# Modulation weights of a two-layer hybrid backbone: pages of four k tiles, selector matmuls for the block sums, other mixing rates

## The chip, the cores and the metric

The kernel runs on one core of one Trainium2 chip. The metric is the device time of one execution in microseconds. Lower is better. Before the change the median of three runs is 1393.65 us (1391.40 to 1397.22).

## What is computed

The reference is a backbone of two layers over 256 latent tokens and 256 context tokens of width 1024, in float32. Each layer has a mixing part (differential attention, a gated linear recurrence and a gated delta rule, four heads each, side by side) and a feed-forward part with a convolution over positions. Ahead of and behind each part the tokens are normalized and modulated. The modulation vectors are what the change is about:

```python
cond_lat = jax.nn.silu(c)[:, None, :]
cond_ctx = jax.nn.silu(c_ctx)
for layer in range(DEPTH):
    mod_l = jnp.split(cond_lat @ ada_w[layer] + ada_b[layer], 6, axis=-1)
    mod_c = jnp.split(cond_ctx @ ada_w[layer] + ada_b[layer], 6, axis=-1)
    p_l = split_cols(modulate(rms_norm(x, norm_g[layer, 0]), mod_l[0], mod_l[1]) @ w_in[layer])
    ...
    x = x + mod_l[2] * rms_norm(mix_l, norm_g[layer, 1])
    ff_l = conv_ffn(modulate(rms_norm(x, norm_g[layer, 2]), mod_l[3], mod_l[4]), ...)
    x = x + mod_l[5] * rms_norm(ff_l, norm_g[layer, 3])
```

So for each layer two vectors of 1024 numbers (one for the latent tokens, one for the context) are multiplied by a matrix of 1024 x 6144, some 25 MB, and a bias is added.

## The kernel before

Tokens lie along the free axis and channels along the 128 partitions. The large products are made of three matmuls each (lines 283 to 285 and 293 to 295), of a high and a low part of weights and activations: ScalarE makes the high part of a weight page (`whi`, line 269), VectorE or GpSimd the low part (`wlo`, line 273). A page is 128 x 1024 float32, 512 KB.

The modulation is computed in blocks of 512 output columns, twelve in a layer. What the first normalization of layer 0 needs (its blocks 0 to 3) is made at the start in eight units of 256 columns by `ada_unit` (line 330), in another form; the other twenty blocks are made by `ada` (line 307). A block reads four pages, each with two of the eight k tiles and 512 columns. The stationary operand is `cs`, the two condition vectors padded to 32 columns, so that a matmul fills only 32 of the 128 output rows. Its place among four column groups of the array is `g = k % 4` (line 316), so that one page fills groups 0 and 1 and the next one groups 2 and 3. When all eight k tiles are in, each group holds the sum over two of them. VectorE copies the bank to SBUF (line 320), four transposes turn it (line 323), a reduction over the four groups adds the partial sums (line 325), and a last instruction adds the bias and writes `mod` (line 326). `ada_unit` already works in the other way: pages of four k tiles and 256 columns (line 337), and a matmul with a selector (line 343), a constant of 128 x 2 that picks row 32 g + s of each group for stream s, so that the matmul adds the four groups itself.

The order of the work is set by generators that `weave` (line 1067) interleaves: each has a rate, and the one that has made the smallest share of its rate goes next. In the mixers of a layer (`mixers`, line 1089) these are the input projections, the delta rule (`gdn`), the recurrence (`hgrn`), attention (`da`) and the modulation blocks, with the rates `RATE[ly][0..4]`; `RATE[ly][5]` is the delta rule's in the stretch before. A scheduler then sets each engine's queue. Layer 0 makes its blocks 4 to 9 in the mixers and blocks 10, 11 and layer 1's blocks 0 to 3 as fill beside the out projection and the first up projections; layer 1 makes blocks 4 to 9 in its mixers and 10 and 11 as fill. The pages of the mixers' blocks use the four `raw` buffers, those of the fill the two `kq` buffers (line 1217).

The delta rule works on two halves of the tokens. For each, and for each of two head pairs, `gA` holds a decay matrix that GpSimd multiplies by beta (line 658), VectorE combines it with the keys' products `kk` (lines 668 to 671) and then solves a triangular system in six levels: matmuls `rt` and `dT` (line 602) with VectorE's updates of `gC` between them (lines 702 to 721). GpSimd also prepares `gF` (line 727) and `gB` (line 729), which are used behind the solve, and the recurrence's `K` (line 930). The level loop of the recurrence copies `K` on ScalarE (`kj`, line 911).

Of the kernel before, what the change touches and what calls it, by code (L numbers as in the profile page):

```python
# [17 lines left out]
AX = mybir.AxisListType  # L18
PSUM = bass.MemoryType.PSUM

P = 128
D = 1024
KT = 8
DEPTH = 2
# [17 lines left out]
    dict(mul=3, add=0, norm=3, lo=1, acc=0, dy=1, dx=8, wlo=2, nxt=2, fill=2, rate=5, hold=1),  # L42
    dict(mul=3, add=0, norm=3, lo=1, acc=0, dy=1, dx=0, wlo=2, nxt=0, fill=2, rate=5, hold=0),
)
RATE = ((121, 197, 32, 218, 37, 8), (53, 64, 15, 50, 5, 7))

GD_Q, GD_K, GD_V, GD_G = 0, 2, 4, 6
HG_Q, HG_G, HG_F, HG_I = 8, 10, 12, 16
# [4 lines left out]
def in_columns():  # L53
    base = np.cumsum([0, 512, 512, 512, 256, 256, 512, 256, 768, 8, 8, 256])
    daq, dak, dav, hgq, hgi, hgf, hgg, gdq, ga, gb, gdg = base[:11].tolist()
    starts = [gdq + 128 * i for i in range(6)] + [gdg, gdg + 128]
    starts += [hgq, hgq + 128, hgg, hgg + 128]
    starts += [hgf + 128 * i for i in range(4)] + [hgi, hgi + 128]
    starts += [dak + 128 * i for i in range(4)]
    starts += [dav + 128 * i for i in range(4)]  # L60
    starts += [daq + 128 * i for i in range(4)]
    ab = []
    for h2 in range(2):
        for kind in (ga, gb):
            for d in range(2):
                for hp in range(2):
                    ab.append(kind + d * 4 + hp * 2 + (h2 ^ hp))
    return starts, ab
# [21 lines left out]
def constants():  # L90
    c = np.zeros((P, C_N), np.float32)

    def put(name, a):
        o, w = C_OFF[name]
        c[:, o:o + w] = a

    i = np.arange(P)
    put("ident", np.eye(P))
    put("ones", 1.0)
    same = (i[:, None] // 64) == (i[None] // 64)  # L100
    put("bones", same)
    put("obones", ~same)
    pm = np.zeros((P, P))
    for m in range(2):
        for d in range(32):
            pm[m * 64 + d + 32, m * 64 + d] = -1.0
            pm[m * 64 + d, m * 64 + d + 32] = 1.0
    put("perm", pm)
    r, j = i[:, None] % 64, np.arange(64)[None]
    put("i64", r == j)  # L110
    big = np.float32(1e30)
    inc = np.concatenate([j >= r, j <= r], 1)
    strict = np.concatenate([j < r, j > r], 1)
    inc, strict = (np.concatenate([t[:, 64:], t[:, :64]], 1) for t in (inc, strict))
    put("inc2", inc)
    put("ninc2", -big * ~inc)
    put("pstr2", big * ~strict)
    hg = []
    for lev in range(LEVELS):
        b = 1 << lev  # L120
        sib = (r // (2 * b)) == (j // (2 * b))
        rl, jl = (r // b) % 2 == 0, (j // b) % 2 == 0
        hg.append(sib & (rl != jl))
    put("hgm", np.concatenate(hg, 1))
    n_freq = 16
    freq = np.float32(10000.0) ** (-np.arange(n_freq, dtype=np.float32) / np.float32(n_freq))
    tok = np.arange(256)
    ang = np.concatenate([(tok // 64).astype(np.float32)[:, None] * freq, (tok % 64).astype(np.float32)[:, None] * freq], -1)
    put("cos", np.cos(ang.T)[i % 32])
    put("sin", np.sin(ang.T)[i % 32])  # L130
    put("eps", EPS)
    put("one", 1.0)
    put("sel", i[:, None] % 32 == np.arange(2)[None])
    put("sel8", i[:, None] % 16 == np.arange(16)[None])
    return c
# [9 lines left out]
class Kernel:  # L145
# [161 lines left out]
    def ada(self, ly, blocks, tags=("raw",), bank="d"):  # L307
        nc = self.nc
        mod = self.mod[ly]
        for j in blocks:  # L310
            ps = self.bank(bank, "ada")
            for kc in range(4):
                w = self.load_raw(self.I["ada_w"][12 * ly + j - 4, kc], 1024, tags[kc % len(tags)]).rearrange("p (k n) -> p k n", k=2)
                for kk in range(2):
                    k = 2 * kc + kk
                    g = k % 4
                    nc.tensor.matmul(ps[32 * g:32 * g + 32, :], self.cs[:, k, :], w[:, kk, :], start=k < 4, stop=k >= 4,  # L317
                                     tile_position=(0, 32 * g))
            st = self.tmp("d2", "adas")
            nc.vector.tensor_copy(st, ps)  # L320
            ps2 = self.bank(bank, "ada2")
            for i in range(4):
                nc.tensor.transpose(ps2[:, 128 * i:128 * i + 128], st[:, i * 128:(i + 1) * 128], self.C("ident"))
            sm = self.small("adr", 8)
            nc.vector.reduce_sum(sm, ps2.rearrange("p (a g s) -> p a s g", a=4, g=4)[:, :, 0:2, :], axis=AX.X)
            nc.vector.tensor_tensor(
                mod[:, 4 * j:4 * j + 4, :], sm.rearrange("p (a s) -> p a s", s=2),
                self.V(ly, "adab", 4 * j, 4 * j + 4).unsqueeze(2).to_broadcast([P, 4, 2]), ALU.add)

    def ada_unit(self, u):  # L330
# [758 lines left out]
    def mixers(self, ly, hT, last, pending):  # L1089
        nc = self.nc  # L1090
        rate = RATE[ly]
        qlo = NCTX if last else 0
# [273 lines left out]
def pack(inp):  # L1366
    f = lambda a: np.ascontiguousarray(np.asarray(a, dtype=np.float32))
    A = {}
    x, ctx = f(inp["x"])[0], f(inp["ctx"])[0]
    tok = np.concatenate([ctx, x], 0)  # L1370
    A["xT"] = f(tok.reshape(NTOK, KT, P).transpose(2, 1, 0))
    cc = np.stack([f(inp["c_ctx"]), f(inp["c"])[0]], -1)
    A["cT"] = f(cc.reshape(KT, P, 2).transpose(1, 0, 2))
    A["consts"] = constants()
    starts, ab = in_columns()
    w = f(inp["w_in"]).reshape(DEPTH, KT, P, -1)
    A["w_in"] = f(np.stack([w[..., s:s + 128] for s in starts], 1).transpose(0, 1, 3, 2, 4)).reshape(DEPTH, N_IN, P, 1024)
    A["w_ab"] = f(w[..., ab].transpose(0, 2, 1, 3)).reshape(DEPTH, P, 128)
    w = f(inp["w_out"]).reshape(DEPTH, KT, P, KT, P)
    A["w_out"] = f(w.transpose(0, 3, 2, 1, 4)).reshape(DEPTH, KT, P, 1024)  # L1380
    w = f(inp["ffn_w_up"]).reshape(DEPTH, KT, P, 44, P)
    A["w_up"] = f(w.transpose(0, 3, 2, 1, 4)).reshape(DEPTH, 44, P, 1024)
    w = f(inp["ffn_w_down"]).reshape(DEPTH, 22, P, KT, P)
    for gi, (f0, fn) in enumerate(GROUPS):
        A[f"w_down{gi}"] = f(w[:, f0:f0 + fn].transpose(0, 3, 2, 1, 4)).reshape(DEPTH, KT, P, fn * P)
    w = f(inp["ada_w"]).reshape(DEPTH, 4, 2, P, 12, 512)
    A["ada_w"] = f(w.transpose(0, 4, 1, 3, 2, 5)).reshape(DEPTH * 12, 4, P, 1024)[4:]
    w = f(inp["ada_w"])[0].reshape(2, 4, P, 6, KT, P)[:, :, :, :2]
    A["ada_w0"] = f(w.transpose(4, 0, 2, 1, 3, 5)).reshape(KT, 2, P, 1024)
    v = np.zeros((DEPTH, P, V_N), np.float32)  # L1390

    def put(ly, name, a):
        o, wd = V_OFF[name]
        v[ly, :, o:o + wd] = a

    cols = lambda a: np.asarray(a).reshape(-1, P).T
    for ly in range(DEPTH):
        put(ly, "g", cols(inp["norm_g"][ly]))
        put(ly, "adab", cols(inp["ada_b"][ly]))
        put(ly, "subln", cols(inp["da_subln_g"][ly]))  # L1400
        put(ly, "lbl", cols(inp["hg_lb_logits"][ly]))
        put(ly, "hgn", np.tile(np.asarray(inp["hg_norm_g"][ly]), 2)[:, None])
        put(ly, "gdn", np.tile(np.asarray(inp["gd_norm_g"][ly]), 2)[:, None])
        put(ly, "cw", np.asarray(inp["gd_conv_w"][ly]).reshape(3, 6, P).transpose(2, 1, 0).reshape(P, 18))
        put(ly, "fw", np.asarray(inp["ffn_conv_w"][ly]).reshape(3, 44, P).transpose(2, 1, 0).reshape(P, 132))
        put(ly, "fb", cols(inp["ffn_conv_b"][ly]))
        for name, src in (("alog", "gd_a_log"), ("dt", "gd_dt_bias")):
            a = np.asarray(inp[src][ly]).reshape(2, 2, 2)
            a = np.stack([np.stack([a[:, hp, h2 ^ hp] for hp in range(2)], 1) for h2 in range(2)], 2)
            put(ly, name, np.concatenate([np.broadcast_to(a[:, :, h2].reshape(1, 4), (64, 4)) for h2 in range(2)], 0))  # L1410
    A["vec"] = v
    A["lam"] = f(np.broadcast_to(f(inp["da_lambda"]).reshape(DEPTH, 1, 256), (DEPTH, P, 256)))
    return A
# [17 lines left out]
```

## Time and profile before

| what | value |
|---|---|
| median of three runs | 1393.65 us (1391.40 to 1397.22) |
| the profiled execution's own time | 1397.04 us |
| span of that execution | 1395.3 us |
| mean granted TensorE clock | 0.974 |
| TensorE busy | 1298.6 us, 93% of the span |
| VectorE, ScalarE, GpSimd busy | 892.5, 658.9, 393.7 us |
| HBM read | 182.14 MB |

The profile is of one execution. The busy table tells which engine has least room. The windows give busy time, granted clock and DMA share of a stretch. The timeline lists instructions of an engine in order; neighbours of one line are put together as x4 or x16, with the time from the first start to the last end, so that the time to the next row's start is what they take of the engine. A float32 matmul shows as two records. The waits name who released an idle engine.

### The profile page before, as it was taken

The page shows a single profiled execution, that of the slowest core. Times are in us where ns is not written, and L with a number is a line of the kernel's source. Part 1 is how long each engine was busy: PE and PEld are TensorE (multiplying, and loading weights), DVE is VectorE, ACT ScalarE, POOL GpSimd, SP SyncE. Part 2 cuts the span into 40 slices and gives each one's busy share as a digit, 9 for nine tenths or more (in the row PEclk, how much of TensorE's full clock was granted, in tenths as well). Part 3 has the DMA queues.
Part 4 walks back from the last instruction along what each step waited for, and adds up shares of the span by engine and source line. Part 5 has one row for each costly group of instructions (what it writes and reads, how often), then busy time and mean ns, then how long its engine had stood idle before and what let it go on. Part 6 is the DMA issues. An engine that isn't in the chain of part 4 may idle for free.

```text
span 1395.3 us, 26653 instructions
## 1 busy us (share of the span) xinstructions
PE 1298.6 (93%) x10720; PEld 1048.0 (75%) x10720; DVE 892.5 (64%) x1722; ACT 658.9 (47%) x1189; POOL 393.7 (28%) x378
## 2 busy tenths in 40 slices
PE   5999997999989999999999997999989998999996
PEld 2768665666677678888888886997666765999995
DVE  3565657877647876434543559877697665776665
ACT  3364424444465544323432455675253354655553
POOL 1012014201046223201210266221241024655553
PEclk8999998999999999999999999999999999999998
DMA  8612443112335663323233234544221265455552
GB/s 300 211 46 91 167 165 139 32 47 76 107 121 189 207 217 115 104 92 105 91 101 96 82 122 135 173 145 155 95 103 34 106 243 181 139 183 185 189 167 76
DMA packets 56283, 185.96 MB, mean 133 GB/s; under 512 B 6368, under 2 KB 10464, under 8 KB 56160
## 3 DMA queue, kind: packets, MB, share of 16 engines
q1 hardware_dynamic: 56160, 184.27, 39.9%
q8 instruction: 84, 1.38, 0.4%
q14 instruction: 39, 0.32, 0.1%
HBM read 182.14 MB, written 2.10 MB: 132 GB/s over the span
## 4 chain that ended last, share of the span: by engine, by line
PE 74%; DVE 12%; ACT 5%; POOL 4%; issue 2%; DMA 2%; SPq 0%; DVEq 0%; POOLq 0%; ACTq 0%
PE up L284 8%; PE up L283 8%; PE up L285 8%; PE in L293 6%; PE in L294 5%; PE in L295 5%; PE dn L285 4%; PE dn L284 4%; PE dn L283 4%; PE ada L317 2%; DVE wlo L273 2%; PE sc L1035 2%; PE op L284 1%; PE op L283 1%; PE op L285 1%
## 5 line engine op out<-in xcount | busy, mean ns | idle before, releaser
L273 DVE TENSOR_TENSOR wlo<-raw,whi 128x1024 fp32r<-128x1024 f32 (+2 forms) x241 | 299.8, 1245 | 269.1 <-issue 90.4
L269 ACT CAST whi<-raw 128x1024 fp32r<-128x1024 f32 (+1 forms) x244 | 248.9, 1023 | 122.6 <-PE dn L285 99.0
L285 PE MATMUL up<-h,whi 128*128 128x256 f32 (+1 forms) x768 | 248.7, 324 | 1.3 <-DVE h L441 0.7
L283 PE MATMUL up<-h,whi 128*128 128x256 f32 (+1 forms) x768 | 248.3, 324 | 1.2 <-ACT h L438 1.1
L284 PE MATMUL up<-h,wlo 128*128 128x256 f32 (+1 forms) x768 | 248.0, 324 | 0.9 <-DVE wlo L273 0.9
L293 PE MATMUL in<-h,whi 128*128 128x512 f32 (+1 forms) x496 | 184.8, 373 | 2.2 <-DVE kq L481 2.2
L273 POOL TENSOR_TENSOR wlo<-raw,whi 128x256 fp32r<-128x256 f32 (+1 forms) x111 | 127.1, 1145 | 173.2 <-ACT whi L269 76.4
L294 PE MATMUL in<-h,wlo 128*128 128x512 f32 (+1 forms) x496 | 175.5, 354 | 0.0
L295 PE MATMUL in<-h,whi 128*128 128x512 f32 (+1 forms) x496 | 175.3, 354 | 0.0
L283 PEld LDWEIGHTS up<-h,whi 128*128 128x128 f32 x768 | 145.8, 190 | 19.6 <-issue 4.2
L285 PEld LDWEIGHTS up<-h,whi 128*128 128x128 f32 x768 | 145.9, 190 | 16.4 <-issue 1.7
L284 PEld LDWEIGHTS up<-h,wlo 128*128 128x128 f32 x768 | 145.9, 190 | 15.5 <-DVE wlo L273 1.9
L284 PE MATMUL dn<-gT,wlo 128*128 128x256 f32 (+1 forms) x400 | 127.6, 320 | 3.4 <-DVE wlo L273 3.4
L283 PE MATMUL dn<-gT,whi 128*128 128x256 f32 (+1 forms) x400 | 127.7, 320 | 2.7 <-ACT gT L300 2.7
L285 PE MATMUL dn<-gT,whi 128*128 128x256 f32 (+1 forms) x400 | 127.3, 320 | 0.5 <-POOL gT L302 0.5
L1262 POOL TENSOR_TENSOR u<-u 128x512 f32<-128x512 f32 (+1 forms) x44 | 44.4, 1010 | 278.3 <-DVE u L481 257.5
L293 PEld LDWEIGHTS in<-h,whi 128*128 128x128 f32 x496 | 96.2, 194 | 19.8 <-issue 5.4
L294 PEld LDWEIGHTS in<-h,wlo 128*128 128x128 f32 x496 | 96.2, 194 | 12.7 <-issue 3.5
L295 PEld LDWEIGHTS in<-h,whi 128*128 128x128 f32 x496 | 95.9, 193 | 12.3 <-issue 1.3
L477 ACT ACTIVATE u<-up,vec 128x256 f32<-128x256 f32 (+1 forms) x96 | 61.8, 644 | 75.2 <-PE up L285 75.2
L284 PEld LDWEIGHTS dn<-gT,wlo 128*128 128x128 f32 x400 | 76.7, 192 | 9.1 <-DVE wlo L273 4.0
L283 PEld LDWEIGHTS dn<-gT,whi 128*128 128x128 f32 x400 | 76.8, 192 | 8.2 <-ACT gT L300 3.1
(281 smaller groups left out, 2318.2 us busy)
## 6 DMA issues: line engine op xcount, KB each, us to landing
raw<-ada_w SPq DMA_DIRECT2D x96, 512.0 KB, 4.4
raw<-w_up SPq DMA_DIRECT2D x96, 512.0 KB, 3.5
raw<-w_in SPq DMA_DIRECT2D x68, 512.0 KB, 3.6
raw<-w_down SPq DMA_DIRECT2D x32, 512.0 KB, 3.5
raw<-w_out SPq DMA_DIRECT2D x24, 512.0 KB, 3.5
raw<-w_down SPq DMA_DIRECT2D x24, 384.0 KB, 3.1
x<-xT SPq DMA_DIRECT2D x16, 256.0 KB, 6.1
x_spill<-x SPq DMA_DIRECT2D x8, 128.0 KB, 2.0
```

Of the source, the lines that this page charges most:

```text
L269: nc.scalar.copy(hi[:, :cols], raw[:, :cols])
L273: e.tensor_sub(lo[:, a:b], raw[:, a:b], hi[:, a:b].bitcast(F32))
L283: nc.tensor.matmul(ps, wh[:, k, :], ah, start=first and k == ks[0], stop=False)
L284: nc.tensor.matmul(ps, wl[:, k, :], ah, start=False, stop=False)
L285: nc.tensor.matmul(ps, wh[:, k, :], al, start=False, stop=last and k == ks[-1])
L293: nc.tensor.matmul(ps, wh[:, k, :], ah, start=k == 0, stop=False)
L294: nc.tensor.matmul(ps, wl[:, k, :], ah, start=False, stop=False)
L295: nc.tensor.matmul(ps, wh[:, k, :], al, start=False, stop=k == n - 1)
L317: nc.tensor.matmul(ps[32 * g:32 * g + 32, :], self.cs[:, k, :], w[:, kk, :], start=k < 4, stop=k >= 4, tile_position=(0, 32 * g))
L477: nc.scalar.activation(dst, ps, AF.Identity, scale=w3[1], bias=bias)
L1035: nc.tensor.matmul(ps[:, :128 * nk], q[64 * m:64 * m + 64, a + 128 * qt:a + 128 * qt + 128], k[64 * m:64 * m + 64, :128 * nk], start=True, ...
L1262: self.nc.gpsimd.tensor_mul(us[0][:, lo:], us[0][:, lo:], us[1][:, lo:])
```

## The change

A page now holds four k tiles of 256 columns, one for each column group; four pages are two column halves by two sets of k tiles. The number and size of the pages stay. The matmuls of a block are chained by manual dependencies that set their order without a semaphore. The transposes and the reduction become four matmuls with the selector, and the bias is added straight from PSUM. Six of the twelve rates are set anew: layer 0's delta rule from 197 to 189, attention from 218 to 221, modulation from 37 to 19; layer 1's projections from 53 to 52, delta rule from 64 to 56, attention from 50 to 26.

```diff
-RATE = ((121, 197, 32, 218, 37, 8), (53, 64, 15, 50, 5, 7))
+RATE = ((121, 189, 32, 221, 19, 8), (52, 56, 15, 26, 5, 7))
...
             ps = self.bank(bank, "ada")
-            for kc in range(4):
-                w = self.load_raw(self.I["ada_w"][12 * ly + j - 4, kc], 1024, tags[kc % len(tags)]).rearrange("p (k n) -> p k n", k=2)
-                for kk in range(2):
-                    k = 2 * kc + kk
-                    g = k % 4
-                    nc.tensor.matmul(ps[32 * g:32 * g + 32, :], self.cs[:, k, :], w[:, kk, :], start=k < 4, stop=k >= 4,
-                                     tile_position=(0, 32 * g))
+            prev = []
+            for i in range(4):
+                half, kc = i // 2, i % 2
+                w = self.load_raw(self.I["ada_w"][12 * ly + j - 4, i], 1024, tags[i % len(tags)]).rearrange("p (k n) -> p k n", k=4)
+                for g in range(4):
+                    x = nc.tensor.matmul(ps[32 * g:32 * g + 32, 256 * half:256 * half + 256], self.cs[:, 4 * kc + g, :], w[:, g, :],
+                                         start=kc == 0, stop=kc == 1, tile_position=(0, 32 * g))
+                    prev = [self._dep(x, prev)]
             st = self.tmp("d2", "adas")
             nc.vector.tensor_copy(st, ps)
             ps2 = self.bank(bank, "ada2")
             for i in range(4):
-                nc.tensor.transpose(ps2[:, 128 * i:128 * i + 128], st[:, i * 128:(i + 1) * 128], self.C("ident"))
-            sm = self.small("adr", 8)
-            nc.vector.reduce_sum(sm, ps2.rearrange("p (a g s) -> p a s g", a=4, g=4)[:, :, 0:2, :], axis=AX.X)
+                nc.tensor.matmul(ps2[:, 2 * i:2 * i + 2], st[:, 128 * i:128 * i + 128], self.C("sel"), start=True, stop=True)
             nc.vector.tensor_tensor(
-                mod[:, 4 * j:4 * j + 4, :], sm.rearrange("p (a s) -> p a s", s=2),
+                mod[:, 4 * j:4 * j + 4, :], ps2[:, 0:8].rearrange("p (a s) -> p a s", s=2),
...
-    w = f(inp["ada_w"]).reshape(DEPTH, 4, 2, P, 12, 512)
-    A["ada_w"] = f(w.transpose(0, 4, 1, 3, 2, 5)).reshape(DEPTH * 12, 4, P, 1024)[4:]
+    w = f(inp["ada_w"]).reshape(DEPTH, 2, 4, P, 12, 2, 256)
+    A["ada_w"] = f(w.transpose(0, 4, 5, 1, 3, 2, 6)).reshape(DEPTH * 12, 4, P, 1024)[4:]
```

How the pages fall among other matmuls shows in TensorE's queue in the fill of layer 0. `up` is an up projection, `ada` a modulation block, the last names are the operands; x2 and x4 are neighbouring matmuls. Before, one of the blocks there:

```order
1875 L284 MATMUL up_4816<-h_4072,wlo_4813 128x256
1876 L317 MATMUL ada_4850<-raw_4851,cs 32x512
1877 L285 MATMUL up_4816<-h_4072,whi_4812 128x256
1878 L283 MATMUL up_4816<-h_4073,whi_4812 128x256
1879 L284 MATMUL up_4816<-h_4073,wlo_4813 128x256
1880 L285 MATMUL up_4816<-h_4073,whi_4812 128x256
1881 L317 MATMUL ada_4850<-raw_4851,cs 32x512
1882 L317 MATMUL ada_4850<-raw_4855,cs 32x512 x2
1883 L283 MATMUL up_4892<-h_4066,whi_4888 128x256
```

And a block at the same place with the change:

```order
1874 L317 MATMUL ada_4898<-raw_4899,cs 32x256 x4
1875 L317 MATMUL ada_4898<-raw_4905,cs 32x256 x4
1876 L283 MATMUL up_4946<-h_4102,whi_4942 128x256
...
1900 L283 MATMUL up_4989<-h_4102,whi_4985 128x256
1901 L317 MATMUL ada_4898<-raw_4911,cs 32x256 x4
1902 L284 MATMUL up_4989<-h_4102,wlo_4986 128x256
...
1910 L283 MATMUL up_4989<-h_4105,whi_4985 128x256
1911 L317 MATMUL ada_4898<-raw_4917,cs 32x256 x4
1912 L284 MATMUL up_4989<-h_4105,wlo_4986 128x256
```

The pages of a block stand apart in both orders. A page that stands alone was two matmuls of 512 columns and is now four of 256.

The second place is GpSimd's queue at the second half of layer 0's delta rule. Lines from 325 on are one lower in the changed file. The two numbers that `gA` and `gB` come with are the two head pairs. Before:

```order
26 L658 TENSOR_TENSOR gA_1983<-gA_1983,sbeta_640 128x512
27 L727 TENSOR_TENSOR gF_2725<-gB_1985,sbeta_640 128x512
28 L729 TENSOR_TENSOR gB_1985<-gB_1985,skd_676 128x256
29 L727 TENSOR_TENSOR gF_2725<-gB_1986,sbeta_640 128x512
30 L729 TENSOR_TENSOR gB_1985<-gB_1985,skd_676 128x256
31 L729 TENSOR_TENSOR gB_1986<-gB_1986,skd_676 128x256 x2
32 L658 TENSOR_TENSOR gA_1984<-gA_1984,sbeta_640 128x512
33 L930 TENSOR_TENSOR K_203_1175<-K_203_1175,F_202_1174 128x128x2x2 x2
```

With the change:

```order
26 L726 TENSOR_TENSOR gF_2702<-gB_1956,sbeta_640 128x512
27 L657 TENSOR_TENSOR gA_1954<-gA_1954,sbeta_640 128x512
28 L728 TENSOR_TENSOR gB_1956<-gB_1956,skd_676 128x256 x2
29 L657 TENSOR_TENSOR gA_1955<-gA_1955,sbeta_640 128x512
30 L929 TENSOR_TENSOR K_203_1175<-K_203_1175,F_202_1174 128x128x2x2 x2
31 L726 TENSOR_TENSOR gF_2702<-gB_1957,sbeta_640 128x512
32 L728 TENSOR_TENSOR gB_1957<-gB_1957,skd_676 128x256 x2
```

The second gA stood behind seven instructions of this half and now stands behind four; a gF, two gB and nothing else moved from ahead of it to behind it, a gF moved ahead of the first gA, and the pair of K now comes ahead of the second gF.

## Rows read from the trace of the kernel before

**Rows 1.** The page's first part: busy us, share of the span, instructions of each engine.
```profile
PE 1298.6 (93%) x10720; PEld 1048.0 (75%) x10720; DVE 892.5 (64%) x1722; ACT 658.9 (47%) x1189; POOL 393.7 (28%) x378
```

**Rows 2.** Busy us by stretch (from:to, length, engines, PEclk, DMA share, GB/s).
```profile
350.00:450.00 100.00, 89.97 (x826) 72.84 (x825) 59.01 (x132) 53.32 (x123) 38.02 (x36) 0.95 0.40 135
450.00:560.00 110.00, 105.13 (x644) 82.48 (x643) 78.84 (x123) 55.73 (x89) 29.71 (x27) 1.00 0.56 185
...
1000.00:1050.00 50.00, 44.90 (x459) 31.49 (x457) 45.20 (x108) 23.11 (x50) 21.09 (x18) 0.93 0.28 96
1050.00:1100.00 50.00, 46.47 (x610) 32.70 (x610) 38.56 (x109) 18.68 (x42) 3.99 (x4) 1.00 0.25 86
```

**Rows 3.** Timeline: an intact block and the next matmul (start us, us, engine, line).
```profile
147.11 1.92 PE L317 MATMUL ada<-raw,cs 128*32 128x512 f32 x16
...
148.97 0.68 PE L602 MATMUL rt<-gC,gA 64*64 64x64 f32 x16
```

**Rows 4.** TensorE's timeline: the first, one middle and the last separate page visit.
```profile
375.89 1.05 PE L317 MATMUL ada<-raw,cs 128*32 128x512 f32 x2
...
445.83 1.05 PE L317 MATMUL ada<-raw,cs 128*32 128x512 f32 x4
446.81 0.38 PE L284 MATMUL op<-mix,wlo 128*128 128x256 f32 x1
...
1181.92 3.16 PE L317 MATMUL ada<-raw,cs 128*32 128x512 f32 x8 [1.52 <-DMA raw<-ada_w]
```

**Rows 5.** TensorE's timeline at the start: one page of four groups, the next matmul.
```profile
37.77 0.64 PE L337 MATMUL ada<-raw,cs 128*32 128x256 f32 x8
38.34 0.50 PE L283 MATMUL in<-h,whi 128*128 128x512 f32 x1
```

**Rows 6.** TensorE's timeline: four transposes of a block, the next matmul.
```profile
176.21 0.60 PE L323 MATMUL ada<-consts,adas 128*128 128x128 f32 x4
176.57 0.47 PE L295 MATMUL in<-h,whi 128*128 128x512 f32 x1
```

**Rows 7.** TensorE's timeline: two selector matmuls; the same without the first record.
```profile
61.90 0.50 PE L343 MATMUL ada<-consts,adas 128*128 128x2 f32 x4
...
61.93 0.47 PE L343 MATMUL ada<-consts,adas 128*128 128x2 f32 x3
62.26 0.48 PE L283 MATMUL in<-h,whi 128*128 128x512 f32 x1
```

**Rows 8.** Instructions on the tile ada: VectorE's reduction (ns min/median/max).
```profile
L325 DVE TENSOR_REDUCE sadr<-ada x20: 142/191/193, 154.2 to 1186.6; 128x8 f32<-128x32 f32 x20
```

**Rows 9.** Waits of TensorE, 215 to 260 us: total us, times, longest.
```profile
PE rt L602 <- DVE gC L707: 8.3, 1, 8.3
PE wt L1052 <- ACT kj L911: 1.6, 1, 1.6
```

**Rows 10.** GpSimd's timeline, second half of layer 0's delta rule.
```profile
214.56 1.05 POOL L658 TENSOR_TENSOR gA<-gA,sbeta 128x512 f32<-128x512 f32 x1 [2.13 <-ACT gA L222]
215.56 3.70 POOL L727 TENSOR_TENSOR gF<-gB,sbeta 128x512 f32<-128x512 f32 x1
219.34 2.63 POOL L729 TENSOR_TENSOR gB<-gB,skd 128x256 f32<-128x256 f32 x1
221.93 2.02 POOL L727 TENSOR_TENSOR gF<-gB,sbeta 128x512 f32<-128x512 f32 x1
223.92 1.87 POOL L729 TENSOR_TENSOR gB<-gB,skd 128x256 f32<-128x256 f32 x3
225.75 1.04 POOL L658 TENSOR_TENSOR gA<-gA,sbeta 128x512 f32<-128x512 f32 x1
```

**Rows 11.** GpSimd's timeline in layer 1: a gF ahead of the second gA.
```profile
1023.69 1.04 POOL L727 TENSOR_TENSOR gF<-gB,sbeta 128x512 f32<-128x512 f32 x1 [2.97 <-ACT gB L544]
```

**Rows 12.** TensorE alone by stretch (busy us, PEclk, DMA share, GB/s), after two waits.
```profile
233.50:243.50 10.00, 10.00 (x117) 0.50 0.18 53
...
258.00:262.00 4.00, 4.00 (x40) 0.50 0.47 133
```

## The prediction, made before the changed kernel ran

> **What bounds the kernel now.** I read the page's busy table first. TensorE is busy 93% of the span [rows 1], so an edit counts by what it adds to TensorE's queue, or by a wait of TensorE that it takes away or makes. Next came busy time by stretch. During the out projection and the first up projections of layer 0, where the modulation blocks of the fill run, TensorE is busy 90.0 of 100 us and 105.1 of 110 us [rows 2]; the 15 us that are left are waits for other engines. Then I read TensorE's timeline at the modulation matmuls, then its waits. One wait stands out: 8.3 us in the mixers of layer 0, where a matmul of the triangular solve waits for VectorE's gC. GpSimd's timeline shows what is behind it.
>
> The sum is made against the profiled execution's own 1397.0 us. That is 3.4 us above the median of the runs, 1393.65 us, so the forecast is the median plus the change in the sum. About 0.5%, 7 us, is what a measurement of this kernel can tell from no change.
>
> **Page matmuls.** A reader of the code would expect two column groups to work at a time before and four after. The rows say otherwise for a block whose four pages are taken one after the other. It has sixteen records (each fp32 matmul is two passes, so two records), and the next matmul starts 148.97 - 147.11 = 1.86 us after the first [rows 3]. A page that is alone holds only two groups, and costs 446.81 - 445.83 = 0.98 us [rows 4], two passes of some 0.43 us and an entry and exit of 0.12 us. Sixteen records in 1.86 us are four times 0.43 us plus 0.14 us: two neighbouring pages already run side by side in four groups. The new form is in the trace as well, in the start's `ada_unit`: eight records, one page of four groups of 256 columns, cost 38.34 - 37.77 = 0.57 us [rows 5], 0.41 us less than the lone page. Four such pages in a row take 4 x 0.43 + 0.14 = 1.86 us. So the eleven blocks that are intact today gain nothing, and only pages that stand alone do.
>
> In the nine other blocks I counted the runs of line 317 in TensorE's timeline, from the one at 375.89 to the one at 1181.92 [rows 4], by passes: 31 times two passes, 31 x 0.86 = 26.7 us. In the new order these nine blocks are 36 pages, four of them torn in two, so 40 x 0.43 = 17.2 us. That saves 9.5 us of TensorE. It lies where TensorE also waits for others [rows 2], and what is saved ahead of such a wait lengthens the wait. The ends are 0 and -9.5 us; I take two thirds, **-6.3 us**.
>
> **Selector matmuls.** Four transposes are four records, and the next matmul starts 0.36 us after the first [rows 6]. Two selector matmuls of `ada_unit` are also four records, with 0.36 us [rows 7]: two columns stream, but each record has its own load of 128x128 weights, and three of them take 62.26 - 61.93 = 0.33 us, 0.11 us each. The change has four selector matmuls, eight records: 0.36 + 4 x 0.11 = 0.80 us, or 0.44 us more a block. Twelve blocks lie in the mixers, where I count it all, 5.3 us; eight in the fill, 3.5 us, where I take two thirds. Together **+7.6 us**, between 5.3 and 8.8.
>
> **VectorE** loses twenty reductions of 0.19 us [rows 8], 3.8 us, and the chain from block sum to `mod` becomes one instruction shorter. No matmul waits for `mod` at these places, so I count nothing. The manual dependencies between matmuls are order only, without a semaphore: nothing. The transfers are the same eighty of 512 KB, from pages of the same row length. On SyncE's queue the blocks of layer 0 move back: two projection weights instead of one go between two blocks, each of which holds all four `raw` buffers until TensorE has used it. TensorE does not wait for those weights in this stretch, so nothing again.
>
> **The rates** change where stages interleave. Counting changes between projection matmuls and others in the two orders gives the same number within two; TensorE's work is the same. What counts is the 8.3 us wait [rows 9]. GpSimd's queue there runs gA of the first head pair, gF, gB, gF, three gB, and only then gA of the second pair, which ends at 225.75 + 1.04 = 226.79 us, 12.2 us after the queue began at 214.56 [rows 10]. VectorE's chain from it to the waiting matmul follows. The new order has gF, gA, two gB, gA: the second gF and two gB come behind. With the prices of this stretch (gF 3.70 and 2.02, mean 2.86; four gB in 2.63 + 1.87, 1.12 each; gA 1.05) that is 2.86 + 1.05 + 2.24 + 1.04 = 7.2 us, **-5.0 us** of the wait. The ends: with the dearest rows, 3.70 + 1.05 + 2 x 2.63 + 1.04 = 11.1 us, a gain of 1.1; with a gF of 1.04 from layer 1 [rows 11] and gB at 1.87 / 3 = 0.62, it is 4.4 us, a gain of 7.8. I take the middle because gF and gB still run in the same stretch beside the same VectorE work.
>
> The Trainium skill, GPSIMD Engine Reference, section 8 (Key points), says that GpSimd shares its SBUF interfaces with VectorE and contends with instructions that have two SBUF inputs; by it the dear rows would hold, the gain would be 1.1 us and the forecast 1391.1 us. Rows 10 show such spread (3.70 against 2.02 for the same gF), and row 11 a gF that did not pay.
>
> The wait has a second price: behind it TensorE is granted 0.50 of its clock, the 1.2 GHz level, for 10 us of full work, a loss of 5.0 us; behind a wait of 1.6 us the same level holds at 258 to 262 us [rows 9, 12], and its loss I put at 3.3 us. If 3.3 us of wait are left, I take **-1.7 us**, between 0 and -5.0.
>
> In layer 1 the second gA now goes ahead of a gF of 1.04 us [rows 11]: **-1.0 us**. TensorE idles 5.1 and 3.5 us in this part of that layer [rows 2]; reordering may win or lose half of it, 4.3 us either way.
>
> **Sum:** -6.3 + 7.6 - 5.0 - 1.7 - 1.0 = -6.4 us, 1390.6 us by the profile's own time and **1387.2 us** as the median.
>
> **Rivals.**
> *The wait goes altogether* (0.24). With the cheap prices gA arrives while TensorE still has work; the wait of 8.3 us and the 5.0 us of half clock are gone. -6.3 + 7.6 - 13.3 - 1.0 = -13.0 us, 1380.6 us. For it: the new order also puts more matmuls ahead of the solve. Against: VectorE's steps behind gA stay.
> *The wait stays in another place* (0.22). The new order takes away one wait and makes another of its size, say for gF, which now comes late for the second pair. Pages and selectors alone: +1.3 us, 1394.9 us.
> *Pages are bound by their transfers* (0.10). The fill's pages go through two buffers. If a page's landing, and not TensorE, sets when the next may be used, the 9.5 us turn into waits, the selectors cost their whole 8.8 us and gA gains its least, 1.1: +7.7 us, 1401.4 us, slower. It decides as soon as most page visits begin with a wait for `raw`. For it: the last visit holds 1.52 us of that [rows 4]; against it: the other two rows there have none.
> *Every page halves* (0.04). If two neighbouring pages ran one after the other today, the eleven intact blocks would fall from 1.86 to 1.00 us as well: 9.4 us more, 1377.8 us. Rows 3 speak against it. The Trainium skill, TensorEngine Tiling (Array Packing), section Overview (Theoretical Speedup), gives up to four times for outputs of 32 columns; the intact blocks already have that.
>
> **Numbers.** The forecast has 0.40, the rivals the rest. Faster by over 0.5% (below 1386.7): 0.24 + 0.04 and nearly half of the forecast's case, 0.47. Slower (above 1400.6): 0.10 and a little of the second rival, 0.13. The rest is 0.40. All gains together (-9.5 + 8.8 - 8.3 - 5.0 - 4.3 = -18.3) would give 1375.3; the range is **1375 to 1400** and leaves out most of the slower case and little else.
>
> **What would show it.** Right: intact blocks still take 1.86 us, lone pages some 0.57 us, eight selector records 0.80 us; GpSimd's second gA ends some 7 us after its first gF starts, the wait ahead of the solve in the mixers of layer 0 is 2 to 5 us, and the half clock after it is shorter. Wrong: intact blocks near 1 us, page visits that begin with waits for `raw`, or a wait over 5 us anywhere in the mixers.

## The result and the profile after

The changed kernel takes 1406.21 us (median of six, 1405.65 to 1407.19) against 1393.88 us before on the same chip (six, 1390.50 to 1399.69): ratio 1.0077, 95% interval 1.0057 to 1.0097. It is **slower**; the forecast was 1387.2 us, and the time lies outside the range of 1375 to 1400.

| | before | after |
|---|---|---|
| the profiled execution's own time, us | 1397.04 | 1407.19 |
| span, us | 1395.3 | 1405.4 |
| mean granted TensorE clock | 0.974 | 0.963 |
| VectorE, ScalarE, GpSimd busy, us | 892.5, 658.9, 393.7 | 888.7, 658.1, 393.2 |

The first part of the page after, against [rows 1]:

```profile
PE 1316.3 (94%) x11120; PEld 1079.4 (77%) x11120; DVE 888.7 (63%) x1702; ACT 658.1 (47%) x1189; POOL 393.2 (28%) x378
```

TensorE is busy 17.7 us longer, where pages and selectors together were booked at 1.3. The prices of the single pieces are not why. TensorE's timeline after, at an intact block, at a lone page and at the selectors, each with the matmul behind it:

```profile
147.38 1.93 PE L317 MATMUL ada<-raw,cs 128*32 128x256 f32 x32
149.25 0.68 PE L601 MATMUL rt<-gC,gA 64*64 64x64 f32 x14
...
173.78 0.95 PE L324 MATMUL ada<-consts,adas 128*128 128x2 f32 x8
174.59 0.48 PE L295 MATMUL in<-h,whi 128*128 128x512 f32 x1
...
449.83 0.64 PE L317 MATMUL ada<-raw,cs 128*32 128x256 f32 x8
450.40 0.38 PE L283 MATMUL op<-mix,whi 128*128 128x256 f32 x1
```

From start to start these are 1.87 us for the block (1.86 forecast), 0.57 us for the lone page (0.57) and 0.81 us for the selectors (0.80), the counterparts of [rows 3 to 6].

The 8.3 us wait of [rows 9] is gone as well. GpSimd's queue after, at the place of [rows 10]:

```profile
216.82 1.22 POOL L726 TENSOR_TENSOR gF<-gB,sbeta 128x512 f32<-128x512 f32 x1 [2.03 <-ACT gB L543]
218.01 1.22 POOL L657 TENSOR_TENSOR gA<-gA,sbeta 128x512 f32<-128x512 f32 x1
219.19 1.75 POOL L728 TENSOR_TENSOR gB<-gB,skd 128x256 f32<-128x256 f32 x2
220.90 1.04 POOL L657 TENSOR_TENSOR gA<-gA,sbeta 128x512 f32<-128x512 f32 x1
```

The second gA ends 5.1 us after the first gF starts; 7.2 was forecast. But TensorE's waits of the same stretch (190 to 260 us; total, times, longest) now read:

```profile
PE kk L601 <- ACT gB L543: 4.1, 1, 4.1
PE kv L601 <- ACT gA L754: 2.3, 1, 2.3
PE wt L1051 <- DVE em L1047: 0.5, 1, 0.5
```

Before, this longer stretch holds, besides the two of [rows 9], one more:

```profile
PE gi L602 <- ACT kq L793: 1.3, 1, 1.3
```

So two new waits of the delta rule (`kk`, its keys' products, and `kv`) stand where one of 8.3 us stood, and the waits listed add up to 6.9 us against 11.2.

**What grew is the clock's share.** The busy row counts time at either level. For each timed execution I multiply its span by the mean granted clock: that is what the span would be if its stretches at 1.2 GHz, waits in them included, took half the time, and the rest of the span is the clock's loss. The table has the averages over the executions of each kernel, for before over all 114 of the study; three executions far longer than all others (1604, 2366 and 4243 us) are left out.

| kernel | executions | ratio to before, 95% | at full clock, us | clock's loss, us |
|---|---|---|---|---|
| before | 114 | | 1362.5 | 30.9 |
| after | 6 | 1.0077 (1.0057 to 1.0097) | 1355.7 | 48.9 |
| new rates alone | 12 | 1.0029 (1.0011 to 1.0048) | 1362.7 | 34.5 |
| new pages and selectors, old rates | 10 | 1.0033 (1.0016 to 1.0051) | 1354.6 | 43.2 |
| new pages alone | 6 | 1.0032 (1.0019 to 1.0044) | 1357.2 | 40.8 |
| selectors alone | 6 | 1.0044 (1.0027 to 1.0062) | 1363.1 | 36.6 |
| selectors alone, 64 columns | 12 | 1.0022 (1.0003 to 1.0041) | 1365.0 | 31.8 |
| pages of the fill alone | 12 | 0.9976 (0.9956 to 0.9997) | 1355.6 | 36.1 |
| pages of the mixers alone | 8 | 1.0048 (1.0026 to 1.0070) | 1365.3 | 35.0 |
| of layer 0's mixers | 12 | 1.0021 (1.0005 to 1.0038) | 1363.2 | 32.5 |
| of layer 1's mixers | 6 | 1.0056 (1.0038 to 1.0073) | 1364.3 | 35.9 |
| layer 0's rates alone | 12 | 1.0012 (0.9997 to 1.0028) | 1362.6 | 32.2 |
| layer 1's rates alone | 12 | 1.0023 (1.0001 to 1.0045) | 1363.5 | 33.3 |
| one rate moved by one | 12 | 0.9970 (0.9954 to 0.9986) | 1359.3 | 30.6 |
| three rates moved a little | 12 | 0.9997 (0.9981 to 1.0013) | 1360.7 | 33.3 |
| fill's pages and one rate moved | 7 | 0.9945 (0.9923 to 0.9967) | 1353.7 | 31.9 |

Counted at full clock the change saves 1362.5 - 1355.7 = 6.8 us; the forecast without its term for the clock said 4.7. The clock takes 48.9 - 30.9 = 18.0 us, where the forecast said -1.7.

The traces give the same split another way, from TensorE's busy time. "Work" is the busy time less half of what lies at 1.2 GHz; that half is the clock's; the rest of the span is idle (us; before and after have a second profile, see below):

| profile | work | clock | idle |
|---|---|---|---|
| before, twice | 1270.0, 1272.0 | 28.6, 22.7 | 96.7, 98.4 |
| after, twice | 1271.0, 1271.6 | 45.2, 42.0 | 89.1, 89.8 |
| new rates alone | 1276.6 | 31.3 | 90.3 |
| new pages and selectors, old rates | 1266.3 | 32.7 | 97.1 |
| new pages alone | 1260.9 | 36.4 | 102.9 |
| selectors alone | 1279.7 | 26.8 | 93.2 |

From the mean of before to that of after, work grows by 0.3 us, idle time falls by 8.1 and the clock takes 18.0 more. Rows of one profile are rougher, since the clock's part differs by 6 us between the two of before.

### The profile page after: what moved, and what is told of

Same layout as the page of the kernel before. It is cut to its first block, busy times and chain, and to the rows that moved or that the text cites. A ratio compares the mean times of both kernels' runs of the same rounds, so it can differ in the third digit from the quotient of the medians.

```text
span 1405.4 us, 27424 instructions
## 1 busy us (share of the span) xinstructions
PE 1316.3 (94%) x11120; PEld 1079.4 (77%) x11120; DVE 888.7 (63%) x1702; ACT 658.1 (47%) x1189; POOL 393.2 (28%) x378
## 5 line engine op out<-in xcount | busy, mean ns | idle before, releaser
L283 PEld LDWEIGHTS up<-h,whi 128*128 128x128 f32 x768 | 147.8, 193 | 14.4 <-ACT h L431 0.9
L285 PEld LDWEIGHTS up<-h,whi 128*128 128x128 f32 x768 | 147.7, 192 | 13.2 <-issue 1.6
L1261 POOL TENSOR_TENSOR u<-u 128x512 f32<-128x512 f32 (+1 forms) x44 | 49.1, 1115 | 282.9 <-DVE u L480 282.9
L295 PEld LDWEIGHTS in<-h,whi 128*128 128x128 f32 x496 | 96.8, 195 | 12.7 <-issue 1.7
```

The lines of the kernel that those rows point to most:

```text
L283: nc.tensor.matmul(ps, wh[:, k, :], ah, start=first and k == ks[0], stop=False)
L285: nc.tensor.matmul(ps, wh[:, k, :], al, start=False, stop=last and k == ks[-1])
L295: nc.tensor.matmul(ps, wh[:, k, :], al, start=False, stop=k == n - 1)
L1261: self.nc.gpsimd.tensor_mul(us[0][:, lo:], us[0][:, lo:], us[1][:, lo:])
```

## Experiments

The first four take the change apart. Theory A was that the new matmul forms lower the clock, theory B that the new order makes TensorE wait elsewhere.

**The rates alone**, on the kernel before:

```diff
-RATE = ((121, 197, 32, 218, 37, 8), (53, 64, 15, 50, 5, 7))
+RATE = ((121, 189, 32, 221, 19, 8), (52, 56, 15, 26, 5, 7))
```

> The kernel before with the new rates alone. Theory A (the clock falls because of the new matmul forms, above all the selectors, which load weights and stream two columns): the order alone costs nothing, the idle time of TensorE falls, so 1386 to 1394 us with a granted clock near 0.974. Theory B (the clock falls because the new order breaks TensorE's work up by other waits): the loss is here, 1400 to 1408 us, clock 0.96 to 0.967.

Measured 1398.81 us, ratio 1.0029: the whole clock loss isn't here, and neither is the gain of 7.7 us that the prediction booked for the rates.

**The new code with the old rates**: the same line the other way, on the kernel after.

> The changed kernel with the old rates. Theory A: the loss is here, 1400 to 1408 us with a clock of 0.96 to 0.967. Theory B: 1390 to 1396 us with the clock of before, since page matmuls and selectors by their rows come out even (some -9 and +9 us). If both this and the rates alone are slower, each by half, the loss is spread over both.

Measured 1399.31 us, ratio 1.0033: at full clock 8 us less than before, with 12 us more clock loss.

**The new pages alone**, with the old transposes, reduction and rates:

```diff
-                nc.tensor.matmul(ps2[:, 2 * i:2 * i + 2], st[:, 128 * i:128 * i + 128], self.C("sel"), start=True, stop=True)
+                nc.tensor.transpose(ps2[:, 128 * i:128 * i + 128], st[:, i * 128:(i + 1) * 128], self.C("ident"))
+            sm = self.small("adr", 8)
+            nc.vector.reduce_sum(sm, ps2.rearrange("p (a g s) -> p a s g", a=4, g=4)[:, :, 0:2, :], axis=AX.X)
```

> Pages of four k tiles, but transposes and reduction, old rates. Both theories: the lone pages save up to 9.5 us of TensorE and nothing is added, so 1384 to 1392 us. If the shorter pages are what costs clock (one form of theory A), 1395 to 1402 us at a clock under 0.97.

**The selectors alone**: the same edit the other way, on the kernel before.

> Old pages, selector matmuls, old rates. By the rows 20 x 0.44 = 8.8 us of TensorE more. Theory B: 1397 to 1403 us with the clock of before (0.974). Theory A in its other form (selectors cost clock): 1405 us and more, clock under 0.967.

Measured 1399.01 and 1401.93 us, 1.0032 and 1.0044. Each part alone is slower, but the two together are not slower than either (1.0033): the parts' ratios do not add up, so neither theory can be settled by subtracting them.

**Dead work ahead of three waits**, on the kernel after. If pauses cause the half clock, filling them should give time back:

```diff
+            self.warm(acc["ps"], a, b, acc.get("warm", 0))
...
+                    if ly == 0 and gi == 2 and a == 256 and m == 2:
+                        self.warm(ps[:, a:b], 0, 256, 6)
```

> The changed kernel with sixteen dead matmuls (128x256 fp32 of constants into a bank that the next real matmul starts anew): four ahead of the wait of 1.9 us near 442 us, six ahead of the wait of 2.6 to 3.5 us near 852 us, six ahead of the wait of 2.97 us near 836 us. At 0.43 us each they are 6.9 us of TensorE. Theory C (the change is lost to granted clock: short waits of TensorE are followed by half clock): the half-clock stretches that began at 445, 858 and 875 us are gone, 1.7 us each, and most dead matmuls lie in the waits, so the time falls below the changed kernel's 1406.2 us, to 1400 to 1405. Rival D (the clock falls whatever TensorE does at these places): the half clock stays and the dead matmuls that don't fit into the waits are added, 1406 to 1410 us.

Measured 1411.64 us (1.0108, 1.0073 to 1.0143): not the 1400 to 1405 us of theory C, though the interval takes in the changed kernel's 1.0077. Waits of TensorE from 830 to 865 us after, and from 830 to 862 us with the dead work:

```profile
PE ss L382 <- POOL acc L403: 3.7, 3, 3.1
PE dn L284 <- DVE wlo L273: 3.4, 2, 3.0
```
```profile
PE ss L390 <- POOL acc L411: 2.7, 2, 2.4
...
PE dn L284 <- DVE wlo L273: 0.9, 2, 0.5
```

The wait for `wlo` took the dead matmuls in, 3.0 to 0.5 us. The wait for `acc` did not: six of them shortened it by 0.7 us, and four ahead of the one near 442 us left it at 2.2 us (1.9 after). So what it waits for came later by most of their time; such a wait is a link of a chain, not room. At full clock the kernel is 7.2 us longer for 6.9 us of dead work (1362.9), and the clock's loss falls by 3.6 only (45.3). In the profile, the stretches at 1.2 GHz of 445 and 875 us are gone as expected and the one of 858 us is still there (854.9 us); but 445 is where the wait stayed. The stretch behind the wait of 4.1 us, which the edit doesn't touch, is 3.4 us instead of 13.7. So this repair fails, and it neither proves nor refutes theory C.

**The fill's saved time put back**, on the new pages alone: the first page of each half is multiplied twice.

```diff
-                for g in range(4):
+                n = 2 if bank == "g" and kc == 0 else 1
+                for r in range(4 * n):
+                    g = r % 4
```

> The new pages alone (transposes, reduction and rates as before), where each first-half page of the eight fill blocks is multiplied twice, the first time for nothing: sixteen visits of 0.43 us, 6.9 us of TensorE, about what the new pages saved there. Theory C (the time saved in the fill turned into pauses and these into half clock): the mean clock goes back from 0.971 toward 0.979 and the time is not above that of the pages alone, 1399.0 us: 1393 to 1399. Rival D (the clock loss belongs to the form of the pages or to their order): clock stays near 0.971 and two thirds or all of the 6.9 us are added, 1403.5 to 1406.

Measured 1403.15 us (1.0050, 1.0029 to 1.0070, against 1.0032, 1.0019 to 1.0044), just below rival D's lower edge. At full clock it is 7.1 us longer than the pages alone (1364.3), and the clock gives 3.7 us back (37.1): theory C fits about half of the work put back. The two intervals overlap, so the half is rough.

**Small changes of the order alone**, on the kernel before: layer 0's fifth rate, 37 to 36; and the delta rule's rates, 197 to 195 and 64 to 63.

> The kernel before with one mixing rate moved by one (layer 0's modulation 37 to 36): a few matmuls change places, no work is added or removed. Theory C: within 2 us of the kernel before, at a clock within 0.003 of its 0.979. Rival E (the kernel before is a lucky order, and any other order of the same work loses clock): 3 to 6 us slower, clock 0.972 to 0.976, as with the new rates alone (1398.8 us, 0.975).

> The kernel before with the delta rule's rates moved a little in both layers (197 to 195, 64 to 63), a larger change of order than the one before, again without added or removed work. Theory C: within 2 us of the kernel before, clock within 0.003. Rival E: 3 to 6 us slower at a clock of 0.972 to 0.976.

Measured 1392.14 us (0.9970) and 1395.79 us (0.9997). The kernel before is no lucky order. But one rate moved by one is worth 0.3% with no work changed, as much as the parts above differ by, and the gain stands at full clock (1359.3 us against 1362.5), not in the clock's loss.

**Selectors with 64 columns**, on the selectors alone; only the first two columns are used:

```diff
-                nc.tensor.matmul(ps2[:, 2 * i:2 * i + 2], st[:, 128 * i:128 * i + 128], self.C("sel"), start=True, stop=True)
+                nc.tensor.matmul(ps2[:, 64 * i:64 * i + 64], st[:, 128 * i:128 * i + 128], self.C("sel", 0, 64), start=True, stop=True)
```

> The selector matmuls alone (old pages and rates), with 64 moving columns instead of 2: the selector's two and the 62 constants that lie behind it; only the first two columns of each product are used. TensorE's time for the eight records stays where the weight loads set it (0.81 us). Theory A1 (the selector costs clock because TensorE streams next to nothing for 0.8 us in a block): clock from 0.974 back to 0.978, time 1395 to 1398. Theory A2 (the selector costs its own time and what it shifts, no clock of its own): as the selectors alone, 1400 to 1403.

Measured 1399.03 us (1.0022; the narrow ones 1.0044), between the two and with overlapping intervals. The edit also moved other matmuls in TensorE's queue, so the columns are not shown to be the reason.

**The fill's pages alone; then the mixers' alone, and each layer's.** The old and the new form of the page loop stand side by side:

```diff
+            if bank == "g":
...
+            else:
```

> The new pages in the eight blocks of the fill alone; the twelve blocks of the mixers, the transposes, the reduction and the rates as before. The pages that stood alone are here, so nearly all of the saving at full clock (span times clock 6 to 7 us less than before). Theory C (what is saved in the fill turns into pauses and half clock): the loss of the new pages is here too, the time is that of the pages alone, 1398 to 1400, clock near 0.971. Rival (the clock is lost in the mixers): the saving stands, 1388 to 1392, clock 0.978.

> The new pages in the twelve blocks of the mixers alone; the fill's blocks, the transposes, the reduction and the rates as before. If the parts add up, this is the pages alone (ratio 1.0032) less the fill's (0.9976): 1.0056, about 7 us slower than before, with the same span times clock and a mean clock near 0.972. If the mixers' pages cost nothing by themselves (the intact blocks take the same 1.86 us) and the loss arises only where both are there: within 2 us of before, clock 0.977.

> The new pages in the six blocks of layer 0's mixers alone. If the fill behind them is what got longer (5.3 us in the profile of both layers' mixers, with a wait of 1.8 us for a page and half clock): 4 to 7 us slower than before and again 3 to 5 us in the stretch from the last out projection to the first down projection of layer 0. If layer 1's mixers carry the loss: within 2 us of before.

> The new pages in the six blocks of layer 1's mixers alone; up to 900 us the program is that of before. If the matmuls that moved in layer 1's mixers carry the loss (4.0 us longer there in the profile of both, 1.3 of it work and 3.2 half clock): 4 to 7 us slower than before, in that stretch. If layer 0 carries it: within 2 us of before. If both have a part: 2 to 4 us each.

Measured 1392.11 us (0.9976), 1401.75 (1.0048), 1397.76 (1.0021) and 1401.73 (1.0056). I had expected the loss in the fill; the fill **gains**, and the mixers' pages lose. Layer 1 has most of it. TensorE's timeline there, in the run with layer 1's pages, at the sixth block (line 318 is the new form):

```profile
1130.72 0.64 PE L318 MATMUL ada<-raw,cs 128*32 128x256 f32 x8 [0.99 <-DMA raw<-ada_w]
1131.89 0.62 PE L318 MATMUL ada<-raw,cs 128*32 128x256 f32 x2 [0.53 <-DMA raw<-ada_w]
1132.44 0.66 PE L1062 MATMUL wt<-consts,em 128*128 128x128 f32 x4
```

The pages here wait 0.99 and 0.53 us for their transfers, which they did not before, and a page is torn: two of its records run alone for 0.55 us. Waits from 1100 to 1150 us, before and in this run:

```profile
PE wt L1052 <- DVE em L1048: 1.8, 2, 1.0
PE do L1060 <- ACT wt L1054: 0.5, 1, 0.5
```
```profile
PE ada L318 <- DMA raw<-ada_w: 1.5, 2, 1.0
PE wt L1062 <- DVE em L1058: 0.8, 1, 0.8
```

The sum is the same, 2.3 us: the waits for pages took the place of others. So the torn page and the waits explain little of the 7.8 us that the ratio makes; the clock has 5.0 of them (35.9 - 30.9). I had expected the stretch of the fill, 5.3 us longer in the profile of both layers' mixers than in the second profile of before, to repeat with layer 0 alone; it was 1.7 us longer.

**Each layer's rates alone**, the line above with one tuple new.

> Only layer 0's three new rates. The prediction's own terms for it (8.3 us wait shorter by 5.0, half clock by 1.7) would give 1388 to 1392. If the loss of the new rates lies here (new waits of 2.3 and 4.1 us at the recurrence and the delta rule, each with half clock behind it), it is 3 to 5 us slower than before, clock 0.975 or less.

> Only layer 1's three new rates. By the prediction 1.0 us less, 4.3 either way. If the loss of the new rates lies here (a fill block moves into the out projection of layer 1, waits of 1.2 and 1.8 us with 10 us of half clock near 1040 us), it is 3 to 5 us slower than before, clock 0.975 or less, and layer 0's rates alone are not slower.

Measured 1397.04 us (1.0012) and 1399.57 us (1.0023). Layer 0's new order by itself, waits from 190 to 260 us:

```profile
PE kk L602 <- ACT gB L544: 4.1, 1, 4.1
PE kv L602 <- ACT gA L755: 2.3, 1, 2.3
PE rt L602 <- DVE gC L721: 1.4, 1, 1.4
```

The first two are the waits of the changed kernel, so the rates make them, not the pages.

**Both kernels a second time**, for a second profile of each.

> The kernel before once more, for a second profile. If the half-clock stretches belong to fixed waits they stand at the same waits as in the first (230, 257, 380, 397, 872, 995, 1039, 1182, 1367 us). If a wait is followed by half clock in one execution and not in another, some are gone and others, as at the waits near 832 and 847 us, are there.

> The changed kernel once more, for a second profile. The same question: the stretches of the first (200, 227, 254, 401, 445, 480, 497, 858, 875, 899, 1002, 1039, 1159, 1183, 1196 us), all or some. Mean clock 0.963 to 0.967, time 1405 to 1408.

TensorE alone by stretch (busy us, granted clock, DMA share, GB/s): before, before again, after, after again.

```profile
890.00:905.00 15.00, 13.06 (x107) 1.00 0.46 150
440.00:450.00 10.00, 8.06 (x53) 1.00 0.66 236
196.00:206.00 10.00, 8.67 (x158) 1.00 0.02 6
1039.30:1049.50 10.20, 9.60 (x118) 0.68 0.53 194
```
```profile
196.00:206.00 10.00, 8.68 (x157) 1.00 0.01 2
440.00:450.00 10.00, 10.00 (x73) 1.00 0.68 236
450.00:560.00 110.00, 105.37 (x625) 1.00 0.55 175
890.00:905.00 15.00, 13.07 (x107) 1.00 0.46 147
```
```profile
440.00:450.00 10.00, 8.05 (x60) 0.83 0.72 225
450.00:560.00 110.00, 103.56 (x739) 0.97 0.58 186
895.00:905.00 10.00, 8.06 (x53) 0.83 0.39 118
...
196.00:206.00 10.00, 7.72 (x87) 0.68 0.75 261
226.90:240.60 13.70, 12.68 (x114) 0.50 0.00 1
1039.30:1049.50 10.20, 9.31 (x77) 0.50 0.39 135
```
```profile
194.00:204.00 10.00, 7.69 (x75) 0.68 0.69 244
440.00:450.00 10.00, 7.92 (x52) 0.83 0.73 231
450.00:560.00 110.00, 104.30 (x733) 0.97 0.57 185
895.00:905.00 10.00, 8.07 (x53) 0.83 0.40 126
```

Their times are 1394.97 and 1405.23 us. Both profiles of before run the stretches at 196, 440, 450 to 560 and 895 us at full clock, both of after partly at 1.2 GHz: behind the new wait of 2.3 us (196 us), at the end of the out projection (440), in the fill (450 to 560), behind waits at the start of layer 1 (895), which before has as well. The stretch near 1040 us at 0.50 stands behind a wait of 1.2 us that was 0.4 before, and one of 1.7 us that before has as well (1.8). The run with layer 1's rates alone has both, and 10 us at half clock, too; before has 6.8 us of it there in its first profile (0.68), none in its second. Outside the start and the end, the half-clock stretches of the trace add up to 51 and 41 us before and 82 and 79 us after. Half of the difference of the means, 17 us, is nearly the clock's 18. Of the nine stretches in the first profile of before six return in the second; of the fifteen of after, thirteen do.

Not each stretch belongs to its wait. The waits near 832 and 847 us, of 3.0 and 2.6 us, have no half clock in the first profile of before. In its second, where they are 3.0 and 3.5 us, both have (TensorE from 822 to 860 us, first and second profile):

```profile
822.00:860.00 38.00, 30.78 (x236) 1.00 0.42 134
```
```profile
822.00:860.00 38.00, 30.37 (x207) 0.91 0.42 133
```

And one stretch of after has no wait ahead of it, at 254.2 us (252.3 in the second profile). TensorE after: the selectors there, and the clock of the ten us ahead and of the stretch; then the ten us in the run with layer 0's rates alone that end just as far behind the four transposes at this place:

```profile
252.03 1.05 PE L324 MATMUL ada<-consts,adas 128*128 128x2 f32 x8
...
244.20:254.20 10.00, 10.00 (x116) 1.00 0.40 149
254.20:257.60 3.40, 3.40 (x54) 0.50 0.47 186
```
```profile
241.50:251.50 10.00, 10.00 (x119) 1.00 0.38 130
251.50:254.90 3.40, 2.00 (x42) 1.00 0.59 241
```

Both profiles of after have this stretch, and so has the run with the dead work (250.8 us); the two runs that have the new rates and the old matmuls (all new rates, and layer 0's alone) don't: there TensorE waits 1.4 us behind the ten us, and the clock stays at 1.00. Here theory A fits better than a wait: the new forms, of pages or of selectors, stand ahead of 3.4 us at half clock, 1.7 us lost. No experiment took the two forms apart at this place.

**The two gains together**, the fill's pages and layer 0's fifth rate at 36:

> The pages of the fill alone together with layer 0's modulation rate moved from 37 to 36. If the two gains found add up (ratios 0.9976 and 0.9970): 0.9946, about 7.5 us faster than before. If they are two draws of where waits fall, no better than either: 0.995 to 1.001.

Measured 1388.61 us against 1395.12: 0.9945, **faster than both kernels**. The saving stays at full clock (8.8 us less than before), and the clock's loss is 31.9 us against 30.9.

## Why the prediction was wrong, step by step

- *Page matmuls, -6.3.* The prices held: in the profile of the pages alone TensorE's work is 10.1 us less than the mean of before, 9.5 counted. But its idle time is 5.4 us more, where a third of 9.5 was allowed for. The fill's pages give 6.9 us at full clock (1362.5 - 1355.6), 5.2 more clock loss, and 3.3 us in time by the ratio (0.4 to 6.1). The claim that **the intact blocks of the mixers gain nothing** held for the blocks, not for the program: their pages alone cost 6.7 us (3.6 to 9.8), and the scheduler puts other matmuls elsewhere around them; how that comes to 6.7 us is shown only as clock (4.1) and 2.8 at full clock, not wait by wait.
- *Selectors, +7.6.* By themselves 6.1 us (3.8 to 8.7), inside the forecast's bounds of 5.3 to 8.8. By the averages the clock has 5.7 of it and full clock only 0.6. In the profile the work grows by 8.7 us, as priced, and idle time falls by over 4. So the price was right, and that the time agrees is luck: the forecast had no clock in it. Beside the new pages they cost nothing measurable (1.0033 with, 1.0032 without).
- *The wait of 8.3 us, -5.0.* **This step failed.** The mechanism on GpSimd was right and better than forecast (5.1 us against 7.2), gF at 1.22 us. But 6.4 us of new waits came, kk's and kv's, close to the second rival, *the wait stays in another place*, whose waits I named wrongly (gF). Nor did the time fall by what the waits lost. The prediction took TensorE's work to be the same under the new rates; in the profile of the rates alone it is 5.6 us more and idle time 7.2 less, and at full clock nothing is left (1362.7 against 1362.5). How waits turned into busy time is not shown. Layer 0's rates alone are 1.7 us slower (0.4 faster to 3.9 slower), where -6.7 was booked.
- *The dear gF.* The Trainium skill, GPSIMD Engine Reference, section 8 (Key points), says that GpSimd contends with VectorE instructions that have two SBUF inputs, and the prediction took from it that the dear gF would stay. The traces fit contention, but they show that either engine may pay: beside the gF of 3.70 us before, VectorE's instructions of this kind are fast, and beside the gF and gA of 1.22 us each after, they are slow (before, then after):

```profile
216.67 0.74 DVE L656 SCALAR_TENSOR_TENSOR gA<-gA,consts 128x256 f32<-128x256 f32 x2
217.67 0.68 DVE L776 TENSOR_TENSOR gB<-gB,kq 128x512 f32<-128x512 f32 x1
```
```profile
216.72 1.60 DVE L655 SCALAR_TENSOR_TENSOR gA<-gA,consts 128x256 f32<-128x256 f32 x2
218.25 1.53 DVE L775 TENSOR_TENSOR gB<-gB,kq 128x512 f32<-128x512 f32 x1
```

- *Half clock behind the wait, -1.7.* **This is the step that decides.** I charged the clock behind one wait and left it as it was everywhere else. Behind the new 4.1 us wait it stays at 0.50 for 13.7 us in both profiles of after; behind the old one of 8.3 it was 13.7 and 10.2 us, the first 3.5 us of them still idle. The other stretches named above came in addition, one of them with no wait at all. The term should have been +18, not -1.7. Without it the forecast said -4.7, and full clock gave -6.8; that these are near is luck in part, since there the rates gave none of the 6.0 us booked for them, and the pages and selectors saved 7.9 where 1.3 more were booked.
- *Layer 1's order, -1.0, either way 4.3.* Its rates alone cost 3.2 us (0.1 to 6.3): inside the bound, on the other side.
- *The rivals.* Pages bound by their transfers gave the side but not the mechanism: four waits for pages, 2.8 us, between 360 and 590 us after, against three and 2.3 us before. No rival had the loss in the granted clock.

What stays open: which part the 18 us belong to, and why the clock falls where it does. The parts' ratios depend on what they are added to (pages 1.0032, selectors 1.0044, both 1.0033; layer 0's and 1's mixers 1.0021 and 1.0056, both 1.0048), and a shift of one rate is worth as much. That the loss is granted clock, at places that both profiles share and most of which stand behind short waits, is shown. That the waits cause it, or that filling them would cure it, is not.

## What to carry to other kernels

Where TensorE is as busy as here (93% of the span), count a change twice: at full clock, and in granted clock behind each wait that the new order makes. Work that TensorE saved among waits was worth about half of itself here, and a new wait of 4.1 us was followed by as long a stretch at 1.2 GHz as an old one of 8.3. Before a part is blamed or praised for 0.3%, move one number of the order by one: here that alone was worth 0.3%.

## What the runs showed of the hardware

- The same wait is followed by 1.2 GHz in one execution and not in another of the same program (the wait of 3.0 us near 832 us).
- A wait of 4.1 us left TensorE at 0.50 for 13.7 us in both profiles of after, though it was busy for 12.7 and 12.3 of them; in the profile with the dead work the same wait was followed by only 3.4 us of it.
- TensorE also fell to 0.50 with no wait ahead: busy for all of ten us, with eight selector records 2.2 us before the fall.
- GpSimd's gF took 3.70 us where VectorE's instructions beside it were fast, and 1.22 us, like the gA behind it, where these took twice as long (0.74 and 0.68 against 1.60 and 1.53 us).
- A selector matmul's time hardly depends on its columns: eight records took 0.81 us with two columns and 0.87 us (176.71 - 175.84 in that run) with 64.
